# Streaming hybrid layer on one core: output weights split early and kept in DRAM, S5 units and their loads moved

## The chip, the cores and the metric

The kernel runs on one core of one Trainium2 chip. Times are device microseconds (us) of one execution. The five engines each take their instructions in order: TensorE (PE) multiplies, VectorE (DVE) and ScalarE (ACT) work elementwise, GpSimd (POOL) works elementwise and issues DMAs of its own, SyncE (SP) issues most of the DMAs. All DMAs run on the core's 16 DMA engines. The metric is the median time of several executions.

## The reference, cut to what matters

```python
h = rms_norm(x, norm_w)                       # x: 4096 prompt frames and 32 sample frames, 1024 wide
p = h @ w_in                                  # split into q/k/v, two gate logits, z_dn, u_s5, z_s5
qkv = silu(causal_conv4(p[:, :1536]))
o_dn = gated_delta_rule(l2(q), l2(k), v, g, beta, s0)   # 4 heads of 128, frames in sequence
o_dn = rms_norm(o_dn, dn_norm_w) * silu(z_dn)
y_s5 = s5_ssm(u_s5, ...)                      # 32 groups of 16, diagonal complex state
gy   = gelu(y_s5)
o_s5 = gy * sigmoid(gy @ glu_w + glu_b) * silu(z_s5)
y = rms_norm(x + concat([o_dn, o_s5]) @ w_out, final_norm_w)
```

All products are made from float16 pairs: a float32 operand is split into a high and a low half (`split`: ACT writes the high half, DVE the low one), and three matmuls of such halves (high by high, high by low, low by high) stand for one.

## The kernel before

The program is traced in Python and every loop is unrolled. A scheduler then lays out each engine's instructions at compile time: it takes the traced order as the priority (`high_priority` with a negative offset makes a block less urgent), and starts an instruction early where its own timing model says that the engine is free and the operands are there. On the chip the order of each engine is fixed: an instruction whose operand is late holds up everything behind it on its engine.

**Phase A** (`phase_a`, 0 to about 925 us of the span) normalizes x and stores it as pairs (`h_d`), splits the weights for it, runs the S5 recurrence (`s5_block`) and stores `gy_d`, and projects the two gate paths z (`zproj`: 24 matmuls of 512 columns for 128 rows, on operands fetched by DMA transposes `hz<-h_d`; line L549 is the transposes, L522 the matmuls). It takes the scale of `w_out` from a first reading (`wstat`). Behind the S5 recurrence it forms the bound of gy (`ma`, an all-partition maximum on POOL, and `pow2` on DVE, L153 to L155), the decay tables (`table`, 33 of them: matmuls L1047, DVE L1049, ACT L1051, a store `dm_d<-tdm`), and `phase_b1` splits the q, k, v and GLU weights and runs the first block of q, k, v. The z projections are traced with `high_priority(offset=-FILL)`, so they fill what the rest leaves of PE.

**Phase B** (`phase_b`) mixes two kinds of work by `Drive`, which keeps the order of PE: the streams of `chunks` (33 chunks of 128 frames in NP = 4 lanes, each urgent by its number) and the stream of `dense` (least urgent). A chunk has a front part (norms, two products, a triangular inverse) and a part that waits for the state S of the chunk before it and ends in L1651, which updates S. `dense` computes q, k, v of 16 blocks of 256 frames (`qkv`, L48 `pp<-h,wk` and so on; operands by DMA transposes in L1349), each allowed once the fronts of two earlier chunks are through, with two S5 output units behind each block while they last:

```python
late = units[len(units) - LATE:]          # 32 units (k, j), LATE = 8
units = units[:len(units) - LATE]
for b in list(range(1, SP)) + [-1] + list(range(SP, NB)):
    if b > 1:
        yield lambda: {2 * b - 4, 2 * b - 3} <= self.front
    yield from self.qkv(b) if b >= 0 else self.qkv_s()
    for u in units[:2] if b >= 0 else [(-1, 0)]:
        yield from self.s5out(*u)
```

With 24 units left by LATE, blocks 1 to 12 take two each and blocks 13 to 15 none; the last 8 follow the last block. Block -1 is the 32 sample frames (`qkv_s`), with a unit of its own.

One **unit** (`s5out`) takes 128 frames: it loads gy (`gyt<-gy_d`, L1446) and the gate (`zr<-z_d`, L1454), both from SP; splits gy into `gh` (L222 on ACT, L223 on DVE); transposes gy (4 matmuls, L52); multiplies by the GLU weight (12 matmuls of 512 columns, `pp<-wg,gh`); and closes with DVE L1462, L1468, L1470, ACT L1469, L1472, POOL L1473 and the store `m5_d<-zr` (L1475, in the trace `m_d<-zr`), which POOL issues. `gyt` and `zr` have two buffers, used in turn (`at = self.nu % 2`), and `gh` has one. `m5` lies in the buffer of `zr`, and the result `t` in that of `gyt`. So a buffer's next gy load can go once L1473 has read it, and the next gate load once the store has landed.

Behind the last block the **tail** follows: `c_weights` loads `w_out` (float32, 1 MB at a time into one staging buffer, L404) and splits it (8 splits, L222 and L223, `wo<-xw`), then the last 8 units, then the output projection of NE = 7 blocks (`out`, L48 `pp<-wo,mx`, transposes L1828 and L1830), while the last chunks run. The memory of the transposed operand `mx` is opened behind that of the staging buffer. **Phase C** does the other blocks of the output when the chunks are through.

Of the kernel before, what the change touches and what calls it, by code (L numbers as in the profile page):

```python
# [6 lines left out]
F32 = mybir.dt.float32  # L7
F16 = mybir.dt.float16
# [3 lines left out]
ALU = mybir.AluOpType  # L12
# [5 lines left out]
H = 4  # L18
# [3 lines left out]
TS = 32  # L22
# [3 lines left out]
FILL = 2000  # L26
# [4 lines left out]
KS = 4096.0  # L31
LATE = 8
SLACK = 1.5
# [46 lines left out]
class Trunk:  # L80
    def __init__(self, ctx, tc, io, T):
# [3 lines left out]
        nc = self.nc  # L85
# [37 lines left out]
        self.be_d = {"p": self.dram.tile([H, self.NC, 128], F32, name="be_d"), "s": self.dram.tile([H, 1, 128], F32, name="bes_d")}  # L123
        self.dm_d = [self.dram.tile([128, H, 128], F32, name=f"dm_d{c}") for c in range(self.NC + 1)]
        self.kp_d = self.dram.tile([16, 2, G, 240], F16, name="kp_d")

# [122 lines left out]
    def phase_a(self):  # L249
# [104 lines left out]
        self.e_gy = cst.tile([128, 2], F32, name="e_gy")  # L354
        self.pow2(ma, self.e_gy[:, 0:1], self.e_gy[:, 1:2])
        self.right.close()
# [7 lines left out]
        with self.tc.high_priority(offset=-250):  # L364
            for ci in order:
                self.table(ci)

        gcf = self.ngC.rearrange("t h c -> t (h c)")
# [670 lines left out]
    def table(self, ci):  # L1039
# [8 lines left out]
        dm = self.tbl.tile([128, H, 128], F32, name="tdm")  # L1048
        nc.vector.tensor_tensor(dm, ps, self.low.unsqueeze(1).to_broadcast([128, H, 128]), op=ALU.add)  # L1049
        for h in range(H):  # L1050
# [96 lines left out]
    def phase_b(self):  # L1147
# [31 lines left out]
        def dense():  # L1179
            units = [(k, j) for k in range(NB // 4) for j in range(8)]  # L1180
            late = units[len(units) - LATE:]
            units = units[:len(units) - LATE]
            for b in list(range(1, SP)) + [-1] + list(range(SP, NB)):
                if b > 1:
                    yield lambda: {2 * b - 4, 2 * b - 3} <= self.front
                yield from self.qkv(b) if b >= 0 else self.qkv_s()
                for u in units[:2] if b >= 0 else [(-1, 0)]:
                    yield from self.s5out(*u)
                if b >= 0:
                    units = units[2:]  # L1190
# [206 lines left out]
    def qkv_s(self):  # L1397
# [35 lines left out]
        yield 0  # L1433

    def s5out(self, k, j):

# [7 lines left out]
        gy = gy.rearrange("p (o i) -> p o i", o=4)[:, :, :m]  # L1444
        if k >= 0:
            nc.sync.dma_start(gy, self.gy_d[k].rearrange("o c t -> c o t")[:, :, 128 * j:128 * j + 128])  # L1446
        else:

            nc.sync.dma_start(gy, self.gys_d.rearrange("o c t -> c o t"))
            g = gh.rearrange("p (o i) -> p o i", o=4)[:, :, :m]  # L1450
            gp.tensor_copy(g.rearrange("p o (i s) -> p o s i", s=8), gy.rearrange("p o (s i) -> p o s i", s=8))
            gp.tensor_copy(gy, g)
        rows = (lambda d: d.rearrange("(i s) d -> s i d", s=8)[j]) if k >= 0 else (lambda d: d)
        nc.sync.dma_start(zr[:m], rows(self.z5_d[k] if k >= 0 else self.z5s_d))  # L1454
        gh = gh.bitcast(F16).rearrange("p (x o i) -> p x o i", x=2, o=4)[:, :, :, :m]
# [18 lines left out]
        dst = self.m5_d[k].rearrange("x (i s) d -> x s i d", s=8)[:, j] if k >= 0 else self.m5s_d  # L1474
        gp.dma_start(dst.rearrange("x t d -> t x d"), m5)  # L1475

    def load_be(self, ci):
# [320 lines left out]
    def c_weights(self):  # L1798
# [5 lines left out]
        self.nc.vector.tensor_scalar(self.uo, self.un["out"], self.em, 2.0 ** -5, op0=ALU.mult, op1=ALU.mult)  # L1804
        with ExitStack() as sc:
            self.wagain("out", self.pool(sc, "c_st", side="right"), self.w_o, 2)
        self.c_mx = self.pool(self.c0, "c_mx", 2, "right")
# [142 lines left out]
```

## Time and profile before

| | us |
|---|---|
| median of 3 runs | 2348.45 |
| runs | 2343.35, 2348.45, 2357.0 |
| the profiled execution | 2354.65 |
| its span in the profile | 2352.8 |
| PE busy | 2068.0 (88%) |
| DVE busy | 1440.2 (61%) |
| ACT busy | 1251.0 (53%) |
| POOL busy | 959.4 (41%) |

The profile is of one execution. Busy time is that of instructions in execution on an engine; where engines wait for each other, the rows tell the releaser, inferred from the semaphores. The granted clock of TensorE is given as a share of full speed: 1.00 is 2.4 GHz throughout a stretch, 0.50 is 1.2 GHz throughout.

### The profile page before, as it was taken

Reading aid. Unit: us, or ns where it says so; the run is one execution under the profiler, and the core shown is the slowest. Engines: PE = TensorE matmul, PEld = TensorE weight load, DVE = VectorE, ACT = ScalarE, POOL = GpSimd, SP = SyncE. Lnnn points to the kernel's source line nnn. Section 1 sums busy time; section 2 is a strip of 40 time slices with the busy share of each in tenths; the row PEclk is TensorE's granted clock in tenths of the full one; section 3 lists DMA queues with packets and bytes.
Section 4 is the critical chain, followed back from the end, with each engine's and each line's share of the span. In section 5 each row is a group of like instructions: output and inputs, shape, how many; then the busy total and the mean of one; then the engine's idle time right before and its main releaser. Section 6 shows DMA issues by size and latency. Waiting matters only on the chain.

```text
span 2352.8 us, 47799 instructions
## 1 busy us (share of the span) xinstructions
PE 2068.0 (88%) x18304; PEld 1492.9 (63%) x18304; DVE 1440.2 (61%) x3289; ACT 1251.0 (53%) x3695; POOL 959.4 (41%) x1444
## 2 busy tenths in 40 slices
PE   4688889888699998698799999989899868999998
PEld 3354677665467554487787778777778755554443
DVE  4685577559466222387687787778777786642223
ACT  5357546543386121376776677667677775431110
POOL 1344225212301012355666666666666675420000
PEclk9899899999899999799899999999999989999999
DMA  6169957765993644323133333322232145455542
GB/s 196 66 175 243 212 116 193 156 54 116 186 235 91 125 114 114 64 59 78 38 79 82 66 80 81 80 62 50 74 82 56 55 146 129 130 165 155 141 139 93
DMA packets 426349, 269.21 MB, mean 114 GB/s; under 512 B 344476, under 2 KB 379384, under 8 KB 425608
## 3 DMA queue, kind: packets, MB, share of 16 engines
q1 hardware_dynamic: 399400, 189.82, 37.1%
q0 software_dynamic: 21968, 67.69, 10.3%
q10 hardware_dynamic: 4752, 8.65, 1.2%
q8 instruction: 143, 2.34, 0.4%
q14 instruction: 86, 0.70, 0.1%
HBM read 102.27 MB, written 86.09 MB: 80 GB/s over the span
## 4 chain that ended last, share of the span: by engine, by line
PE 43%; issue 11%; ACT 7%; DMA 7%; DVE 6%; POOL 4%; SPq 1%; DVEq 0%; POOLq 0%; ACTq 0%
PE pp L48 23%; PE pz L522 9%; PE bk L48 7%; DMA gyt<-gy_d 3%; PE bk L52 2%; DVE acc L1384 2%; ACT jk L1555 2%; DMA dm_d<-tdm 1%; PE pt L1047 1%; DMA hz<-h_d 1%; DVE kn L1667 1%; DMA ab_d<-abt 1%; SPq L1349 1%; ACT acc L1382 1%; ACT br L1642 1%
## 5 line engine op out<-in xcount | busy, mean ns | idle before, releaser
L522 PE MATMUL pz<-wz,hz 128*128 128x512 f16 (+1 forms) x1464 | 385.7, 389 | 27.6 <-DMA hz<-h_d 25.5
L1384 DVE SCALAR_TENSOR_TENSOR acc<-pp,cwu,acc 128x256 f32<-128x256 f32 x540 | 252.9, 477 | 67.4 <-ACT acc L1382 60.6
L48 PEld LDWEIGHTS <-mx 128*128 128x128 f16 (+1 forms) x1584 | 152.3, 98 | 177.2 <-issue 1.6
L522 PEld LDWEIGHTS <-hz 128*128 128x128 f16 (+1 forms) x1464 | 143.4, 99 | 187.3 <-DMA hz<-h_d 33.3
L48 PE MATMUL pp<-h,wk 128*128 128x259 f16 (+1 forms) x1632 | 222.7, 276 | 0.1
L530 PE MATMUL pp<-wa,ht 128*128 128x260 f16 x1536 | 196.3, 284 | 27.1 <-ACT wa L222 10.4
L48 PE MATMUL pp<-h,wq 128*128 128x259 f16 (+1 forms) x1632 | 214.6, 273 | 0.5 <-DVE acc L1384 0.5
L48 PE MATMUL pp<-h,wv 128*128 128x259 f16 (+1 forms) x1632 | 209.9, 272 | 1.0 <-DVE acc L1384 1.0
L48 PE MATMUL po<-wo,mx 128*128 128x512 f16 (+1 forms) x912 | 197.2, 379 | 0.3 <-ACT acc L1219 0.3
L530 PEld LDWEIGHTS <-ht 128*128 128x128 f16 x1536 | 153.7, 101 | 57.1 <-issue 23.9
L48 PEld LDWEIGHTS <-wk 128*128 128x128 f16 x1632 | 156.5, 100 | 35.9 <-issue 8.8
L48 PEld LDWEIGHTS <-wq 128*128 128x128 f16 x1632 | 152.4, 99 | 27.6 <-issue 5.5
L48 PEld LDWEIGHTS <-wv 128*128 128x128 f16 x1632 | 148.5, 98 | 22.6 <-issue 1.6
L48 PE MATMUL pp<-wo,mx 128*128 128x512 f16 x672 | 152.0, 379 | 0.0
L556 POOL DMA_DIRECT2D z_d<-zt x64 | 36.8, 576 | 260.2 <-DVE zt L555 217.4
L1845 ACT ACTIVATE junk<-xt 128x1024 bf16<-128x1024 f32 (+1 forms) x19 | 20.1, 1056 | 176.4 <-issue 92.6
L48 PE MATMUL pp<-wg,gh 128*128 128x512 f16 (+1 forms) x396 | 104.2, 391 | 6.4 <-ACT gh L222 3.4
L555 DVE SCALAR_TENSOR_TENSOR zt<-zt,pz 128x512 f32<-128x512 f32 (+1 forms) x66 | 44.9, 680 | 102.0 <-ACT zt L554 101.3
L1382 ACT ACTIVATE acc<-pp,cwu 128x256 f32<-128x256 f32 x180 | 84.8, 482 | 38.6 <-PE pp L48 38.0
L48 PEld LDWEIGHTS <-a 128*128 128x128 f16 x1320 | 78.2, 98 | 37.3 <-issue 28.3
L1844 DVE SCALAR_TENSOR_TENSOR xt<-po,uo,xt 128x512 f32<-128x512 f32 (+1 forms) x38 | 28.5, 749 | 116.7 <-PE po L48 116.6
L948 POOL DMA_DIRECT2D gy_d<-vv x128 | 67.7, 535 | 78.7 <-ACT vv L943 40.3
(615 smaller groups left out, 5011.1 us busy)
## 6 DMA issues: line engine op xcount, KB each, us to landing
xn<-in_x SPq DMA_DIRECT2D x32, 512.0 KB, 4.5
h_d<-hl POOLq DMA_DIRECT2D x32, 512.0 KB, 5.4
z_d<-zt POOLq DMA_DIRECT2D x64, 256.0 KB, 3.6
xt<-in_x SPq DMA_DIRECT2D x18, 512.0 KB, 4.3
out_y<-xt SPq DMA_DIRECT2D x18, 512.0 KB, 3.6
dm_d<-tdm ACTq DMA_DIRECT2D x33, 256.0 KB, 3.7
dm<-dm_d SPq DMA_DIRECT2D x33, 256.0 KB, 2.9
gy_d<-vv POOLq DMA_DIRECT2D x128, 64.0 KB, 3.9
```

Source lines behind the costliest of these rows:

```text
L48: return self.nc.tensor.matmul(out, lhs, rhs, start=start, stop=stop)
L52: return self.nc.tensor.transpose(out, src, ident)
L522: self.nc.tensor.matmul(ps, a[x][:, c], w[:, y, c], start=c == 0 and x == y == 0, stop=c == K - 1 and x == 1)
L530: self.nc.tensor.matmul(pu[hf][:, :260], ht[x][:, c, :m], self.w_a[:, y, c, 260 * hf:260 * hf + 260], start=c == 0 and x == y == 0, stop=c ...
L555: nc.vector.scalar_tensor_tensor(zt, zt, 1.0, pz, op0=ALU.add, op1=ALU.mult)
L556: nc.gpsimd.dma_start(rows(dst[0][blk]) if blk >= 0 else dst[1], zt)
L948: gp.dma_start(gy[s], gn[16 * s:16 * s + 16, :, :128])
L1047: nc.tensor.matmul(ps[:, h], self.ident[:k, p:p + 1].to_broadcast([k, 128]), gc, start=True, stop=True)
L1382: nc.scalar.activation(acc, ps[:, 0:n], AF.Copy, scale=cw[:, e, 0:1])
L1384: v.scalar_tensor_tensor(acc, ps[:, j:j + n], cw[:, e, j:j + 1], acc, op0=ALU.mult, op1=ALU.add)
L1555: act.activation(junk, src[:, h], AF.Square, accum_out=out[:, h:h + 1])
L1844: v.scalar_tensor_tensor(xt[:m, sl], ps, self.uo[:m], xt[:m, sl], op0=ALU.mult, op1=ALU.add)
```

## The change

1. `w_out` is split in phase A. Behind the decay tables, at the low priority of the z projections, eight pieces are loaded by SP (two staging buffers), split by ACT and DVE into one buffer `ho`, and stored by POOL into a DRAM tensor `wo_d`. `c_weights` then only loads the finished pairs from it, eight DMAs of 512 KB on SP, with no staging buffer. The new pool `b_wo` (12 KB in each partition) lies behind the pools of the tables in SBUF and is closed with them.
2. The `pow2` of the S5 bound is traced behind the tables and its first instruction is tied behind the last table's DVE instruction.
3. LATE goes from 8 to 4, and four units (EARLY) are traced ahead of block 2, before the wait for the fronts of chunks 0 and 1. Blocks 1 to 12 still take two units each, and four remain for the tail.
4. The loads of a unit stand in `s5load`. The first four units load at their own start, from SP, as before. From the third unit on, a unit ends with the loads for the unit two behind it (`useq` is the order of all 33): the gy load issued by POOL, behind the unit's own store, and the gate load by SP.

```diff
--- before.py
+++ after.py
@@ -29,7 +29,8 @@
 SB = 2
 Z0 = 3
 KS = 4096.0
-LATE = 8
+LATE = 4
+EARLY = 4
 SLACK = 1.5
 
 
@@ -122,6 +123,7 @@
         self.m5s_d = self.dram.tile([2, TS, 512], F16, name="m5s_d")
         self.be_d = {"p": self.dram.tile([H, self.NC, 128], F32, name="be_d"), "s": self.dram.tile([H, 1, 128], F32, name="bes_d")}
         self.dm_d = [self.dram.tile([128, H, 128], F32, name=f"dm_d{c}") for c in range(self.NC + 1)]
+        self.wo_d = [self.dram.tile([128, 2, 1024], F16, name=f"wo_d{k}") for k in range(8)]
         self.kp_d = self.dram.tile([16, 2, G, 240], F16, name="kp_d")
 
 
@@ -352,7 +354,6 @@
         v.tensor_single_scalar(mx, mx, 91.0, op=ALU.add)
         ma = self.allmax(mx, 1, "g")
         self.e_gy = cst.tile([128, 2], F32, name="e_gy")
-        self.pow2(ma, self.e_gy[:, 0:1], self.e_gy[:, 1:2])
         self.right.close()
         self.tbl = self.pool(bld, "b_tbl", 3)
         self.pt = self.pool(bld, "b_pt", 2, psum=True)
@@ -364,6 +365,17 @@
         with self.tc.high_priority(offset=-250):
             for ci in order:
                 self.table(ci)
+
+        wp = self.pool(bld, "b_wo")
+        with self.tc.high_priority(offset=-FILL):
+            for k in range(8):
+                f = wp.tile([128, 1024], F32, name="xo", bufs=2)
+                hl = wp.tile([128, 2, 1024], F16, name="ho")
+                nc.sync.dma_start(f, io["w_out"][:, k])
+                self.split(hl[:, 0], hl[:, 1], f, self.ws["out"][:, k:k + 1])
+                nc.gpsimd.dma_start(self.wo_d[k], hl)
+        self.after(v.tensor_single_scalar(ma, ma, 2.0 ** -100, op=ALU.max), self.last_tdm)
+        self.pow2(ma, self.e_gy[:, 0:1], self.e_gy[:, 1:2])
 
         gcf = self.ngC.rearrange("t h c -> t (h c)")
         mark = self.last_exp
@@ -1046,7 +1058,7 @@
             p = h * n + c
             nc.tensor.matmul(ps[:, h], self.ident[:k, p:p + 1].to_broadcast([k, 128]), gc, start=True, stop=True)
         dm = self.tbl.tile([128, H, 128], F32, name="tdm")
-        nc.vector.tensor_tensor(dm, ps, self.low.unsqueeze(1).to_broadcast([128, H, 128]), op=ALU.add)
+        self.last_tdm = nc.vector.tensor_tensor(dm, ps, self.low.unsqueeze(1).to_broadcast([128, H, 128]), op=ALU.add)
         for h in range(H):
             self.last_exp = nc.scalar.activation(dm[:, h], dm[:, h], AF.Exp, bias=self.ngC[:, h, ci:ci + 1])
             self.after(self.last_exp, self.last_gelu)
@@ -1178,9 +1190,14 @@
 
         def dense():
             units = [(k, j) for k in range(NB // 4) for j in range(8)]
+            self.useq = units[:2] + [(-1, 0)] + units[2:]
             late = units[len(units) - LATE:]
             units = units[:len(units) - LATE]
             for b in list(range(1, SP)) + [-1] + list(range(SP, NB)):
+                if b == 2:
+                    for u in units[:EARLY]:
+                        yield from self.s5out(*u)
+                    units = units[EARLY:]
                 if b > 1:
                     yield lambda: {2 * b - 4, 2 * b - 3} <= self.front
                 yield from self.qkv(b) if b >= 0 else self.qkv_s()
@@ -1432,6 +1449,14 @@
             self.blk[-1, nm] = dst[:, H * i:H * i + H]
         yield 0
 
+    def s5load(self, k, j, at, eng):
+        m = 128 if k >= 0 else TS
+        gy = self.rm["gyt"][:, at].rearrange("p (o i) -> p o i", o=4)[:, :, :m]
+        eng.dma_start(gy, self.gy_d[k].rearrange("o c t -> c o t")[:, :, 128 * j:128 * j + 128] if k >= 0 else
+                      self.gys_d.rearrange("o c t -> c o t"))
+        rows = (lambda d: d.rearrange("(i s) d -> s i d", s=8)[j]) if k >= 0 else (lambda d: d)
+        self.nc.sync.dma_start(self.rm["zr"][:m, at], rows(self.z5_d[k] if k >= 0 else self.z5s_d))
+
     def s5out(self, k, j):
 
 
@@ -1442,16 +1467,13 @@
         gy, zr, gh = self.rm["gyt"][:, at], self.rm["zr"][:, at], self.rm["gh"][:, 0]
         t, m5 = gy, zr
         gy = gy.rearrange("p (o i) -> p o i", o=4)[:, :, :m]
-        if k >= 0:
-            nc.sync.dma_start(gy, self.gy_d[k].rearrange("o c t -> c o t")[:, :, 128 * j:128 * j + 128])
-        else:
-
-            nc.sync.dma_start(gy, self.gys_d.rearrange("o c t -> c o t"))
+        if self.nu <= 4:
+            self.s5load(k, j, at, nc.sync)
+        if k < 0:
+
             g = gh.rearrange("p (o i) -> p o i", o=4)[:, :, :m]
             gp.tensor_copy(g.rearrange("p o (i s) -> p o s i", s=8), gy.rearrange("p o (s i) -> p o s i", s=8))
             gp.tensor_copy(gy, g)
-        rows = (lambda d: d.rearrange("(i s) d -> s i d", s=8)[j]) if k >= 0 else (lambda d: d)
-        nc.sync.dma_start(zr[:m], rows(self.z5_d[k] if k >= 0 else self.z5s_d))
         gh = gh.bitcast(F16).rearrange("p (x o i) -> p x o i", x=2, o=4)[:, :, :, :m]
         self.split(gh[:, 0], gh[:, 1], gy, self.gs)
         pt = self.pb.tile([128, 512], F32, name="pp")[:m]
@@ -1473,6 +1495,8 @@
         gp.tensor_tensor(m5[:, 1], t, m5[:, 0], op=ALU.subtract)
         dst = self.m5_d[k].rearrange("x (i s) d -> x s i d", s=8)[:, j] if k >= 0 else self.m5s_d
         gp.dma_start(dst.rearrange("x t d -> t x d"), m5)
+        if 2 < self.nu < len(self.useq) - 1:
+            self.s5load(*self.useq[self.nu + 1], at, gp)
 
     def load_be(self, ci):
 
@@ -1802,8 +1826,8 @@
         self.w_o = wt.tile([128, 2, 8, 1024], F16, name="wo")
         self.uo = wt.tile([128, 1], F32, name="uo")
         self.nc.vector.tensor_scalar(self.uo, self.un["out"], self.em, 2.0 ** -5, op0=ALU.mult, op1=ALU.mult)
-        with ExitStack() as sc:
-            self.wagain("out", self.pool(sc, "c_st", side="right"), self.w_o, 2)
+        for k in range(8):
+            nc.sync.dma_start(self.w_o[:, :, k], self.wo_d[k])
         self.c_mx = self.pool(self.c0, "c_mx", 2, "right")
 
     def phase_c(self):
```

## Rows read from the trace of the kernel before

**Rows 1.** Stretches: PE, PEld, DVE, ACT, POOL busy; PE's clock; DMA share; GB/s.

```profile
700.00:925.00 225.00, 224.96 (x1449) 134.18 (x1447) 82.81 (x202) 70.00 (x152) 28.73 (x53) 1.00 0.49 114
925.00:951.00 26.00, 4.89 (x145) 4.42 (x141) 6.40 (x9) 5.38 (x18) 14.84 (x23) 0.62 0.73 131
951.00:1027.00 76.00, 63.15 (x575) 49.48 (x576) 39.51 (x95) 38.11 (x120) 27.35 (x41) 0.86 0.23 43
1027.00:1885.00 858.00, 783.07 (x9183) 681.15 (x9180) 650.62 (x1565) 618.09 (x1997) 552.46 (x788) 0.97 0.29 69
1885.00:1962.00 77.00, 51.83 (x483) 37.80 (x480) 63.35 (x110) 53.06 (x147) 51.37 (x55) 0.82 0.62 167
1962.00:2110.00 148.00, 147.85 (x1123) 82.47 (x1120) 82.09 (x166) 62.56 (x181) 58.87 (x85) 0.99 0.47 125
```

**Rows 2.** ACT's waits, 1027 to 1885 us: total us, times, longest.

```profile
ACT gh L222 <- DMA gyt<-gy_d: 45.3, 11, 6.6
```

**Rows 3.** Timeline of one S5 buffer from 1188 us: start, length, engine, line.

```profile
1188.22 1.15 POOL L1473 TENSOR_TENSOR zr<-gyt,zr 128x512 f16<-128x512 f32 x1
...
1189.39 0.36 SPq L1446 DMA_DIRECT2D gyt<-gy_d  x1
...
1189.66 0.77 POOL L1475 DMA_DIRECT2D m_d<-zr  x1 [0.30 <-POOL zr L1473]
...
1192.32 0.72 ACT L222 ACTIVATE gh<-gyt,gs 128x512 f16<-128x512 f32 x1 [1.34 <-DMA gyt<-gy_d]
```

**Rows 4.** Timelines of SP, POOL and ACT at a longer stall, from 1306 us.

```profile
1306.98 10.19 SPq L1349 DMA_TRANSPOSE h<-h_d  x1
1317.27 0.52 SPq L1446 DMA_DIRECT2D gyt<-gy_d  x1
...
1312.54 1.16 POOL L1473 TENSOR_TENSOR zr<-gyt,zr 128x512 f16<-128x512 f32 x1 [1.81 <-ACT zr L1472]
...
1322.63 0.72 ACT L222 ACTIVATE gh<-gyt,gs 128x512 f16<-128x512 f32 x1 [6.58 <-DMA gyt<-gy_d]
```

**Rows 5.** PE's waits, 1027 to 1885 us, the two longest in total.

```profile
PE bk L48 <- DVE T L1716: 12.2, 15, 2.7
PE bk L48 <- ACT tp L1519: 7.2, 6, 3.3
```

**Rows 6.** POOL's store of a unit, 1027 to 1885 us: busy, mean ns.

```profile
L1475 POOL DMA_DIRECT2D m_d<-zr x22 | 16.4, 747 | 3.6 <-POOL zr L1473 3.6
```

**Rows 7.** DMA issues: size of each, median us to landing.

```profile
vb<-z_d POOLq DMA_DIRECT2D x32, 256.0 KB, 3.0
...
xn<-in_w_out SPq DMA_DIRECT2D x8, 512.0 KB, 5.9
```

**Rows 8.** The tail's output weights by tile: ns min/median/max, first and last start.

```profile
L48 PE MATMUL pp<-wo,mx x112: 376/379/379, 1968.7 to 1999.9; 128*128 128x512 f16 x112
...
L223 DVE SCALAR_TENSOR_TENSOR wo<-xw,ws_out,wo x8: 1273/1281/2172, 1904.3 to 1943.2; 128x1024 f16<-128x1024 f32 x8
```

**Rows 9.** The chain that ended last, its longest piece: start, us, what.

```profile
2110.75 33.67 PE pp L48 x156
```

**Rows 10.** DVE's updates of the state by chunks 20, 24 and 31.

```profile
1730.43 1.11 DVE L1651 SCALAR_TENSOR_TENSOR S_p<-S_p,egl,bk 128x128 f32<-128x128 f32 x4
...
1847.55 1.11 DVE L1651 SCALAR_TENSOR_TENSOR S_p<-S_p,egl,bk 128x128 f32<-128x128 f32 x4
...
2110.85 1.11 DVE L1651 SCALAR_TENSOR_TENSOR S_p<-S_p,egl,bk 128x128 f32<-128x128 f32 x4
```

**Rows 11.** Timelines of SP and ACT at the sample unit, from 937 us.

```profile
937.38 9.21 SPq L1349 DMA_TRANSPOSE h<-h_d  x1
...
951.25 0.40 ACT L222 ACTIVATE gh<-gyt,gs 128x128 f16<-128x128 f32 x1 [16.06 <-POOL gyt L1452]
```

**Rows 12.** Timeline of PE at the decay tables, from 626 us.

```profile
626.34 2.08 PE L1047 MATMUL pt<-gcp,ident 128*128 128x128 f32 x8 [16.34 <-DVE tdm L1049]
...
644.03 6.00 PE L1047 MATMUL pt<-gcp,ident 128*128 128x128 f32 x32 [4.24 <-DVE mm L155]
```

## The prediction

> **What bounds the kernel now.** I read the busy time by stretches first. From 700 to 925 us PE is never idle and its clock is full; from 1962 to 2110 us nearly so. Between them three stretches lose time [rows 1]: the start of the chunks (925 to 1027 us, PE busy 68 of 102 us at clocks of 0.62 and 0.86), the long middle (1027 to 1885 us, busy 783 of 858 us at 0.97), and the head of the tail (1885 to 1962 us, busy 52 of 77 us at 0.82). Elsewhere only PE's work counts, so a gain is idle time or half-speed time taken out of one of these three, and a loss is time put into a stretch where PE is full.
>
> Then the waits. In the middle ACT stands still 45.3 us in all for a gy load, 11 times, up to 6.6 us [rows 2]: the next block's first split of gy stands in ACT's order right behind where the load was thought to land. In the tail the output weights are what is late: the last low half starts at 1943.2 us, and the first output matmul only at 1968.7 us [rows 8]. At the start the sample unit's split holds ACT for 16.06 us: SP is busy 9.21 us with a transpose before it issues the small load [rows 11].
>
> **The tail.** At a clock of 0.82 the 51.83 us of PE in its first 77 us are some 42.5 us of full-speed work; 34.5 us are lost [rows 1]. The change takes out the eight splits, the staging buffer's four rounds, and four of eight units. What is left is eight loads of 512 KB. A load of that size of the same weights took 5.9 us to land [rows 7]; the DMA's 167 GB/s of this stretch [rows 1] would move 4.2 MB in 25 us, so the weights are there some 25 us into the stretch, near 1910 us, instead of 1944 us. The transposes of `mx` no longer wait for the staging buffer, but go behind these loads on SP. I take the first output matmul at 1915 us. A unit's 12 matmuls cost 2.6 us, at 33.67/156 = 0.216 us each [rows 9], so eight units are 21 of the 42.5 us and the chunks' work the rest, 0.28 us per us. In 30 us there are then 10.4 us of units and 8.4 us of chunks: 11 us lost. PE's work from 1885 us to the end of the chunks is 42.5 + 0.99 x 147.85 = 189 us; less 10.4 moved away it is 178.5, and with 11 us lost it ends at 2075 us instead of 2110 us.
>
> That holds only if the chunks are through by then. Chunk 31 ends at 2110.85 us, and phase C opens behind it [rows 10]. From chunk 20 to 24 a chunk took 29.3 us; from 24 to 31, with the outputs between, 37.6 us. Seven chunks at 29.3 us end at 2053 us, at 37.6 us where they end now. With 10 us less of other work and no splits in ACT's and DVE's order I take 33.5 us: 2082 us. So **tail: -28 us**, from -47 (PE loses nothing: 2063 us) to 0 (the present pace).
>
> **The start.** Four units go there. Their PE work is 10.4 us, against 102 - 0.62 x 4.89 - 0.86 x 63.15 = 45 us lost there now [rows 1]. But most of this is lost before the sample unit's load lands at 951 us, and that load keeps its place behind SP's transpose. The four units come after it, two buffers in turn; each brings ACT a split that can wait. If each waits as in the middle (45.3/11 = 4.1 us) and none of the PE work is absorbed, they cost 27 us; if all fits, nothing. After 951 us some 22 us are lost (76 - 0.86 x 63.15), so half of the work should fit, with a few us of waiting: **+8 us**, bounds 0 and +27.
>
> **The middle.** Is the load earlier? L1473 frees the buffer at 1189.4 us, and SP issues the load there and then; POOL would issue the store first, at 1189.66 us for 0.77 us, and the load behind it [rows 3]. In the longer stall the buffer was free at 1313.7 us and SP, in its transpose until 1317.2 us, issued at 1317.27 us; the split started at 1322.63 us [rows 4]. So the load goes out up to 3 us earlier where SP was held and about 1 us later where it was not: nearly the same on the mean. "Two units ahead" is where it stood already. What may change is the split's place in ACT's order, since the plan now sees a store and a load on POOL ahead of it; that can take perhaps half of 45.3 us of standing. PE's two longest waits on what ACT and DVE do behind it come to 19.4 us [rows 5], which is the most that I give this. Against it stands POOL's own time: a gy load of 512 runs, where the unit's store of 256 rows holds POOL 0.747 us [rows 6], so about 1.2 us for each of 22 units, 26 us on an engine busy 552 of 858 us [rows 1]; PE's two longest waits name no POOL instruction, so most of it is covered, and without the cover it is at worst a third, 8 us. A load issued by POOL is no slower by itself: `vb<-z_d` lands in 3.0 us [rows 7]. The gate load still waits on SP for the store to land, with the next transposes and the chunks' loads behind it, as before. **-7 us**, from -19 to +8.
>
> The Trainium skill (DMA: Bandwidth & Descriptors, section Issuing engines are not separate DMA queues) speaks against this part: starting DMAs on several engines "will only save the time on the sequencer it takes to initiate the DMA". The trace agrees as far as it goes, since SP's issue took 0.36 us [rows 3]; by that rule the middle would stand at nothing and the sum below at -18.
>
> **Phase A.** The early splitting brings eight times 1.28 us to DVE [rows 8], about as much to ACT, eight loads on SP, eight stores on POOL and 8.4 MB to the DMAs. Each store waits on POOL for both halves of its split, with the stores of z behind it; each load from the third on waits on SP for a staging buffer, with the transposes for z behind it. ACT is busy 70 and DVE 83 of 225 us there, so the engines have room; PE has none, and any z projection that comes late costs in full [rows 1]. Operands are two ahead, 24 x 0.216 = 5.2 us each, which covers short holds. The tables before it already make PE wait 16.34 us behind their stores and 4.24 us behind a small DVE operation of the bound's group [rows 12]; with the bound and what hangs on it behind the tables the 4.24 us may go. I set one short hold of 6 us against 4: **+2 us**, from -4 to +20 (three rounds each late by one projection's 5.2 us, and 4 us more). The moved bound itself costs nothing: its users are the units and the chunks' scales, all behind the tables. `b_wo` gives its memory to phase B's pools, whose first tiles must wait for the last store; that is covered as long as the splits end before 925 us.
>
> **Sum**: -28 + 8 - 7 + 2 = -25 us. The profiled execution took 2354.65 us, 6 us above the median of 2348.45 us; from 2354.65 it gives 2330, and as a median **2323 us**.
>
> **Rivals** (times as medians).
> The stalls of the middle go entirely, and the four units fit in the start: -28 - 19 + 2 = -45, 2303 us. For it: each stall sits on one load alone [rows 2]. Against it: the buffer is freed no earlier. 0.15.
>
> The queue doesn't matter: POOL's issue changes neither landing nor ACT's order, so that the change does not do in the middle what it says; -28 + 8 + 2 = -18, 2330 us. For it, the load that SP issues as the buffer comes free [rows 3]; against it, the one that SP holds [rows 4]. 0.12. It is what the Trainium skill's page DMA: Bandwidth & Descriptors would make of the move.
>
> The chain of chunks bounds the tail: outputs start earlier, but chunk 31 ends no sooner, at 37.6 us a chunk, and PE runs dry before phase C. 0 + 8 - 7 + 2 = +3, 2351 us. For it: that pace [rows 10]. Against it: PE was full there, and the pace was 29.3 us with full blocks of q, k, v between. 0.15.
>
> The other side, slower: the staging of `w_out` sits in SP's order ahead of transposes for z. SP waits for a staging buffer until the split before it, and PE has one projection's cover. With a load of 5.9 us [rows 7], a split of 2.6 (two halves like DVE's) and a store of the same size as the load, a round is 14.4 us, so a full hold costs 14.4 - 5.2 = 9 us; six rounds wait so (two buffers are free at first): 55 us, and -25 - 2 + 55 = +28, 2376 us. At three rounds it is level with before, from five slower by over 0.5%. For it: PE has no idle time there; against it: engines with two thirds idle time split promptly. 0.08.
>
> **Numbers.** The forecast has 0.50. A difference under 0.5%, 12 us, is about what a measurement here cannot tell from none. Faster by more: forecast, first and second rival, 0.50 + 0.15 + 0.12 = 0.77; the same: the third, 0.15; slower 0.08. The range is 2288 to 2352 us: below the first rival by most of the tail's own bound, above up to the third's; the slower rival and a little at the low end stay out.
>
> **What would show it.** Right: the first `pp<-wo,mx` within 35 us of the last block of q, k, v; no `wo<-xw` behind phase A; chunk 31 about 28 us sooner after chunk 24; ACT's wait on gy loads in the middle cut but not gone; the stretch from 700 us to the first dm load not longer than 225 us. Wrong: PE idle between the last early output and phase C (third rival), waits of PE on hz in phase A (fourth), ACT held 4 us or more by each early unit between 951 and 1027 us, or POOL as the releaser of PE's waits in the middle.

## The result, and the profile after

The changed kernel takes 2321.97 us (median of four runs, 2318.2 to 2327.94) against 2347.88 us before: a ratio of 0.9872, 95% interval 0.9845 to 0.9899. The profiled execution took 2318.2 us with a span of 2316.5 us, 36.3 us less than the profiled one before. Part of these 36 us is no effect of the change, as will be seen.

The stretches of the changed kernel, cut at its own marks; columns as in [rows 1]:

```profile
700.00:925.00 225.00, 223.08 (x1439) 131.58 (x1438) 90.92 (x234) 72.97 (x155) 34.14 (x64) 1.00 0.56 130
925.00:951.00 26.00, 4.80 (x142) 4.33 (x137) 8.07 (x9) 5.21 (x18) 14.35 (x20) 0.64 0.86 133
951.00:1051.50 100.50, 80.59 (x733) 59.83 (x734) 59.10 (x128) 55.40 (x171) 48.16 (x66) 0.91 0.29 71
1051.50:1881.00 829.50, 775.87 (x9151) 680.71 (x9150) 660.63 (x1564) 614.60 (x1977) 566.50 (x804) 0.98 0.32 71
1881.00:1923.00 42.00, 27.58 (x268) 20.09 (x266) 26.16 (x57) 26.25 (x81) 30.07 (x39) 0.79 0.92 247
1923.00:2109.00 186.00, 184.67 (x1376) 102.34 (x1376) 95.34 (x202) 74.19 (x226) 68.85 (x101) 0.99 0.44 118
```

Busy time times clock is full-speed work; the rest of a stretch is lost. In the start 50 of 126.5 us are lost, against 45 of 102 before; in the middle about 69, against 98; from the last block to phase C 24 of 228, against 39 of 254 (clocks have two digits, so the middle is good to some 4 us, the others to about 1). The start holds 19 us more work: the four units and what of blocks and chunks came with them. The tail holds 11 us less. The row of the tail before, from its last block to phase C:

```profile
1891.80:2145.60 253.80, 228.31 (x1703) 130.81 (x1702) 151.33 (x283) 115.83 (x325) 109.22 (x145) 0.94 0.55 151
```

ACT's wait for gy loads in the middle (total, times, longest), 45.3 us in [rows 2]:

```profile
ACT gh L224 <- DMA gyt<-gy_d: 7.9, 8, 2.1
```

PE's long wait at the tables, 626.34 us in [rows 12], ends here at

```profile
618.68 2.08 PE L1059 MATMUL pt<-gcp,ident 128*128 128x128 f32 x8 [15.19 <-DVE tdm L1061]
```

The tail: the output matmuls and weight loads by tile (ns min/median/max, first and last start), DVE's longest wait in its head, SP's loads of the gate and the last chunk's update:

```profile
L49 PE MATMUL pp<-wo,mx x672: 376/380/635, 1923.0 to 2107.2; 128*128 128x512 f16 x168
L1830 SPq DMA_DIRECT2D wo<-wo_d x8: 602/771/4829, 1883.1 to 1893.5; - x8
```

```profile
DVE zr L1484 <- DMA zr<-z_d: 7.3, 1, 7.3
```

```profile
1918.53 1.04 SPq L1458 DMA_DIRECT2D zr<-z_d  x2
...
2102.70 1.12 DVE L1675 SCALAR_TENSOR_TENSOR S_p<-S_p,egl,bk 128x128 f32<-128x128 f32 x4
```

All eight weight loads are issued by 1893.5 us, and at 11.6 to 16.2 us to landing they are there near 1910 us. The first output matmul starts at 1923.0 us. Last come the gate loads of two units: the stores that free their buffers go out at 1892.22 and 1897.73 us, but SP, in the transposes of `mx` for some 23 us, issues them at 1918.53 us, and DVE and then PE (5.8 us) wait for them. Chunk 31 ends 8 us earlier than in [rows 10], but only 6 us ahead of phase C (2109 us), where before it was 35 us (2145.6 us).

### The profile page after: what moved, and what is told of

Read it like the earlier page. It is cut to its first block, busy times and chain, and to the rows that moved or that the text cites. A ratio compares the mean times of both kernels' runs of the same rounds, so it can differ in the third digit from the quotient of the medians.

```text
span 2316.5 us, 47857 instructions
## 1 busy us (share of the span) xinstructions
PE 2053.1 (89%) x18304; PEld 1486.0 (64%) x18304; DVE 1443.1 (62%) x3290; ACT 1250.8 (54%) x3695; POOL 983.3 (42%) x1481
## 4 chain that ended last, share of the span: by engine, by line
PE 39%; issue 10%; DVE 9%; ACT 5%; DMA 4%; POOL 4%; SPq 0%; DVEq 0%; POOLq 0%; ACTq 0%
PE pp L49 23%; PE bk L49 8%; PE pz L534 5%; PE bk L53 2%; DVE acc L1401 2%; ACT jk L1579 1%; DMA gyt<-gy_d 1%; DVE kn L1691 1%; DMA hz<-h_d 1%; PE po L49 1%; DVE gyt L1492 1%; DMA h<-h_d 1%; DMA dm_d<-tdm 0%; ACT acc L1399 0%; DVE ubd L1746 0%
## 5 line engine op out<-in xcount | busy, mean ns | idle before, releaser
L49 PE MATMUL pp<-h,wk 128*128 128x259 f16 (+1 forms) x1632 | 217.5, 272 | 0.1
L1579 ACT ACTIVATE jk<-bk 128x128 bf16<-128x128 f32 x264 | 74.9, 284 | 38.9 <-PE bk L53 33.1
```

Source lines behind the costliest of these rows:

```text
L49: return self.nc.tensor.matmul(out, lhs, rhs, start=start, stop=stop)
L1579: act.activation(junk, src[:, h], AF.Square, accum_out=out[:, h:h + 1])
```

## The experiments

All were compared with the kernel before on the same chip (its medians there 2356 to 2361 us), so ratios count. Two theories of the middle: **place** (the gain comes from where the split of gy stands in ACT's order) and **queue** (it comes from the load's move off SP). This table, from PE's timelines, cuts each profile at the same events: the end of PE's long wait at the tables; the last z matmul; the first matmul of block 3; the last of v of block 15; the first of phase C. The column "lost in the tail" is the tail less PE's busy time in it times its clock. All but the ratio is in us. Where an expectation names a time, it reckons from the 2348 us of the result, so a run's ratio times 2348 us is what it has to be held against.

| run | ratio | phase A | start | middle | tail | lost in the tail | ACT's gy waits |
|---|---|---|---|---|---|---|---|
| before | 1 | 297.8 | 102.8 | 864.9 | 253.8 | 39 | 45.3 |
| the change | 0.9872 | 305.3 | 127.5 | 829.5 | 228.1 | 24 | 7.9 |
| E1 tie alone | 0.9932 | 296.5 | 103.1 | 847.0 | 254.2 | 38 | 0 |
| E2 change, loads on SP | 0.9953 | 306.9 | 117.7 | 857.9 | 227.5 | 25 | 36.1 |
| E3 part 4 alone | 0.9934 | 295.2 | 100.9 | 853.1 | 258.8 | 42 | 15.9 |
| E4 change, no early units | 1.0011 | 307.8 | 102.3 | 856.2 | 256.3 | 38 | 15.7 |
| E5 change, no part 1 | 0.9920 | 297.9 | 127.6 | 837.3 | 240.9 | 40 | 8.5 |
| E6 change, units in blocks 13, 14 | 0.9891 | 310.1 | 101.6 | 860.1 | 230.3 | 29 | 15.0 |
| E7 tie and LATE 4 | 0.9872 | 296.9 | 101.8 | 858.3 | 236.2 | 38 | 0 |
| E8 change and tie | 0.9889 | 305.9 | 127.1 | 835.5 | 230.8 | 30 | 0 |
| E9 change, SP, tie | 0.9831 | 309.6 | 117.5 | 825.2 | 230.2 | 29 | 0 |
| E10 E7, part 1 behind the tables | 0.9881 | 311.8 | 99.1 | 863.5 | 221.4 | 16 | 0 |
| E11 E10 with LATE 2 | 0.9880 | 311.5 | 100.4 | 863.5 | 221.7 | 17 | 0 |
| E12 E9 without part 1 | 0.9943 | 297.1 | 117.7 | 852.5 | 239.9 | 38 | 0 |

The intervals are within 0.002 to 0.004 of the ratio. From phase C to the end it is 207 to 208 us in every run. PE's wait at the tables ended between 618.7 (the change) and 634.5 us (E1). Up to there PE, ACT and POOL run the same instructions in the same order in every profile, before and after: what stands ahead of it varies from one execution to the next, and 7.7 of the 36.3 us between the two profiles came from there.

**E1, the place alone.** In the kernel before:

```diff
-                        nc.scalar.activation(dst, dst, AF.Copy, scale=self.sq["p"])
+                        self.qmark = nc.scalar.activation(dst, dst, AF.Copy, scale=self.sq["p"])
...
-        self.split(gh[:, 0], gh[:, 1], gy, self.gs)
+        self.split(gh[:, 0], gh[:, 1], gy, self.gs, marks=(self.qmark, None))
```

> The kernel before with one edit: each unit's high half of gy is ordered on ACT behind the last q of the block before it; loads, queues, unit places and output weights are untouched. First theory (place): the middle gained because ACT no longer stands at a gy load that has just gone out, so the tie alone takes ACT's 45.3 us of such waits below 10 us and PE's lost time between the start of block 2 and the last block from about 99 us to about 70: 2348 - 25 to 30 = 2318 to 2323 us. Rival (queue): the gain came with the load's move off SP; then ACT's waits go, but PE stays where it was, 2343 to 2350 us.

2342.36 us, 0.9932 (0.9909 to 0.9954). ACT's 45.3 us of waits are gone, the middle is 17.9 us shorter, the other stretches stay. With no load moved, the tie is worth 16 us of time (2332 us on the scale of the expectation), half of what the changed middle shows: less than the place theory asked for and more than the queue theory allowed. The tie also changes the rest of the plan (see E12), so E1 alone does not show that the whole gain comes from the waits.

**E2, the queue undone.**

```diff
-            self.s5load(*self.useq[self.nu + 1], at, gp)
+            self.s5load(*self.useq[self.nu + 1], at, nc.sync)
```

> The changed kernel with the two-ahead gy loads issued by SP instead of POOL. Place theory: the time follows where the split stands on ACT. If it comes back to right behind the load, ACT's waits come back towards 45 us and the middle is up to 30 us longer, 2335 to 2352 us; if it stays where it is, 2317 to 2327 us, though SP issues the loads up to 10 us late behind its transposes. Queue theory: loads are held on SP by transposes and by waits for the units' stores, ACT waits as before wherever the split stands, 2340 to 2352 us.

2348.19 us, 0.9953 (0.9925 to 0.998), 2337 us on the scale of the expectation; its interval reaches into the ranges of both theories, so the time does not decide. ACT's waits in the middle are back:

```profile
ACT gh L224 <- DMA gyt<-gy_d: 36.1, 10, 5.4
```

Yet SP holds these loads no more than POOL did: in the middle they go out within 2.3 us of L1495's end (POOL's in the change 1.0 to 3.1 us behind it), and the split stands again right behind where they land. So place again, and the middle is 28 us longer. But the start is 10 us **shorter** than with POOL. Most of that is work that stands elsewhere: the start of the change, then that of E2:

```profile
924.00:1051.50 127.50, 86.39 (x897) 64.93 (x897) 67.17 (x137) 61.20 (x189) 62.51 (x85) 0.85 0.41 83
```

```profile
935.50:1053.20 117.70, 80.32 (x818) 60.67 (x818) 64.64 (x121) 53.26 (x155) 53.83 (x73) 0.81 0.39 83
```

E2 does 79 matmuls less there, 65 us of full-speed work against 73; 53 us are lost against 54. POOL's issue does come later: POOL issues a load of the change behind the unit's store and other work (POOL's timeline; the buffer is free when L1495 ends):

```profile
976.67 1.16 POOL L1495 TENSOR_TENSOR zr<-gyt,zr 128x512 f16<-128x512 f32 x1
977.79 1.15 POOL L1715 TENSOR_TENSOR a<-br,bd 128x512 f16<-128x512 f32 x1
978.90 1.15 POOL L1719 TENSOR_TENSOR al<-br,ah 128x512 f16<-128x512 f32 x1
...
980.47 0.77 POOL L1497 DMA_DIRECT2D m_d<-zr  x1
981.23 0.77 POOL L1455 DMA_DIRECT2D gyt<-gy_d  x1
```

and SP in E2, 0.03 and 0.6 us behind the end of L1495:

```profile
986.16 0.36 SPq L1455 DMA_DIRECT2D gyt<-gy_d  x1
...
990.20 0.38 SPq L1455 DMA_DIRECT2D gyt<-gy_d  x1
```

**E3, part 4 alone** (LATE 8, no early units, output weights and bound as before).

```diff
-LATE = 4
-EARLY = 4
+LATE = 8
+EARLY = 0
...
-        for k in range(8):
-            nc.sync.dma_start(self.w_o[:, :, k], self.wo_d[k])
+        with ExitStack() as sc:
+            self.wagain("out", self.pool(sc, "c_st", side="right"), self.w_o, 2)
```

> The kernel before with the loads two ahead alone (gy by POOL): LATE is 8, no early units, output weights and the bound as before. Both theories of the middle: about 30 us of PE's lost time go there and nothing else changes, 2315 to 2325 us, as quick as the whole change. The forecast's own size for this part was -7 us, 2341 us. If the middle gained in truth because work was moved into the start, nothing, 2345 to 2352 us.

2345.54 us, 0.9934 (0.991 to 0.9958). The middle gives 11.8 us, not 30, and there the forecast's -7 us was the nearer. The time, 2332 us on the scale of the expectation, lies between the two. The tail is 5 us longer with these loads.

**E4, no early units.**

```diff
-LATE = 4
-EARLY = 4
+LATE = 8
+EARLY = 0
```

> The changed kernel without the early units: LATE 8, EARLY 0; the other parts stay. Theory that the 25 us by which block 2 comes later are mostly work moved there (19 us) from the middle and the tail, and 5 us more of lost time: block 2 starts near 953 us again, the tail has four units more (10 us of PE) and the middle what else had moved, 2317 to 2325 us. Rival, that the early units simply hold up the start by 25 us: 2322 - 25 + 10 = 2307 us. Second rival, that without them the tail loses its head start: the tail is 10 us of units and up to 11 us of lost time longer, 2330 us or more.

2359.83 us, 1.0011 (0.9986 to 1.0035): all that was gained is gone, and only the second rival comes near. The tail is as long as before although the weights are split early, because the outputs are traced behind the units: the first output matmul starts 80.4 us behind the last block, as the last unit's L1484 ends (1977.26 to 1978.01 us). The stretch, and PE's longest wait in it, which ends at 1940.33 us and is for a gate load that SP issues behind the transposes of `mx`:

```profile
1897.60:1978.00 80.40, 55.52 (x496) 37.91 (x495) 51.42 (x106) 44.88 (x137) 51.33 (x70) 0.83 0.68 174
```

```profile
PE pp L49 <- DVE zr L1484: 9.2, 1, 9.2
```

So with eight units part 1 buys nothing in the tail, and costs 10 us in phase A.

**E5, no part 1.** The pool `b_wo` is left out, and `c_weights` loads and splits as before:

```diff
-                self.split(hl[:, 0], hl[:, 1], f, self.ws["out"][:, k:k + 1])
-                nc.gpsimd.dma_start(self.wo_d[k], hl)
...
-        for k in range(8):
-            nc.sync.dma_start(self.w_o[:, :, k], self.wo_d[k])
+        with ExitStack() as sc:
+            self.wagain("out", self.pool(sc, "c_st", side="right"), self.w_o, 2)
```

> The changed kernel without part 1: the output weights are loaded and split behind the last block, as before; the early units, the loads two ahead and the moved bound stay. Theory that the tail's gain comes from its four units fewer, and that part 1 costs phase A about 10 us (from the end of PE's long wait at the tables to the last z matmul 305 to 308 us with it, 295 to 298 without): phase A is 9 us shorter, and the tail at most 13 us longer if the weights (54 us behind the last block, before) take the place of the four units (42 us): -9 to +4 us against the change, a ratio of 0.983 to 0.989. Rival, that the weights bound the tail, as the forecast had it: the tail is as long as before less the four units' 10 us of work, +15 us less the 9: a ratio of 0.990 or more.

2343.7 us, 0.992 (0.9897 to 0.9942): the rival's ratio. Phase A is 7.4 us shorter and the tail 12.8 us longer, as the theory had it, which is 5 us; the rest of the 11 us lies in a middle 7.8 us longer, with the same tracing there. The tail's 12.8 us, against "at most 13" and "15", cannot tell the two apart, but its rows can. DVE's splits, and the tails of E4 and of this run to phase C:

```profile
L224 DVE SCALAR_TENSOR_TENSOR wo<-xw,ws_out,wo x8: 1269/1280/3625, 1912.9 to 1949.7; 128x1024 f16<-128x1024 f32 x8
```

```profile
1897.60:2153.90 256.30, 230.10 (x1703) 131.19 (x1702) 133.78 (x271) 108.14 (x316) 109.09 (x152) 0.95 0.57 149
```

```profile
1896.10:2137.00 240.90, 216.57 (x1647) 126.13 (x1646) 138.10 (x265) 111.00 (x318) 104.58 (x142) 0.93 0.55 146
```

The last unit's last GLU matmul starts at 1936.8 us, the last split at 1949.7 us and the first output matmul at 1957.4 us, 61 us behind the last block: with four units left, late weights (and the transposes of `mx`, which SP issues behind their loads, from 1942.84 us on) are what comes last, as the rival has it. Early weights alone (E4) leave 38 us of the tail lost and fewer units alone 40 us, against 39 us before; only the two together, as in the change, bring it to 24. What fewer units alone take off the tail is work done elsewhere.

Phase A at 297.9 us with the moved bound says that part 2 costs nothing. It gains nothing either: the 4.24 us of [rows 12] are gone, but PE's waits at the tables come to 22.1 us in all, with 15.9 in the long one, against 21.6 with 16.3 before.

**E6, the four units in blocks 13 and 14.**

```diff
-EARLY = 4
+EARLY = 0
```

> The changed kernel with EARLY 0 and LATE 4: the four units go to blocks 13 and 14 instead of ahead of block 2. Against the run without early units (LATE 8, ratio 1.001) the tail should be 28 us shorter, as it is in the change. Theory that the start gives the early units room for nothing: in the middle PE is full, they cost there their 10 us of work and the time is 18 us better than without, a ratio of 0.993. Rival, that the middle has room as well (PE idle 53 to 61 us there): 28 us better, 0.989.

2336.26 us, 0.9891 (0.9872 to 0.991): the rival's figure. Against E4 the tail is 26 us shorter and the middle only 4 us longer. Units need not go into the start. That the middle has room in general is not shown: the same move makes it 11 us longer in E7 than in E1.

**E7, tie and LATE 4.** The two edits of E1 in the kernel before, and

```diff
-LATE = 8
+LATE = 4
```

> The kernel before with two edits of a line each: the tie of the gy split on ACT behind the last q of the block before (alone 0.993), and LATE 4, so that four units go from the tail to blocks 13 and 14. Nothing is split early, no queue is changed. If the number of units sets the tail: the tail 25 us shorter less up to 13 us for the weights, the middle 18 us shorter by the tie and up to 10 us longer by the units: -20 to -33 us, a ratio of 0.986 to 0.9915. Rival, that the weights, split as late as before, bound the tail: only the units' 10 us move, nothing is gained on the sum, and the ratio is that of the tie, 0.993 to 0.995.

2330.0 us, 0.9872 (0.9846 to 0.9899): these lines alone are as fast as the whole change. With late weights the tail is 17.6 us shorter, but 38 us of it are lost, as before; the middle holds the units' work and is 11 us longer than in E1.

**E8, change and tie** (the edits of E1 in the changed kernel).

> The changed kernel with the tie added. Place theory: ACT's last 8 us of waits on gy loads in the middle go, with little behind them, 0 to -8 us against the change: a ratio of 0.984 to 0.987. Rival, that the change's middle gained by the queue as well as by the place, and the tie only moves the split later than its user needs it: the same or worse, 0.987 to 0.990.

2336.17 us, 0.9889 (0.9865 to 0.9914), not to be told from the change: the rival's figure, though the interval reaches the place theory's. The last 8 us of ACT's waits were worth nothing that can be seen.

**E9, change, loads on SP, tie** (the edits of E1 and E2 in the changed kernel).

> The changed kernel with the two-ahead gy loads on SP, as in the run that was 0.995, and with the tie of the gy split on ACT. Place theory: the SP loads cost only because the split stood right behind them again (ACT waited 36 us); with the tie the stretch from the last z matmul to the last block is as long as in the change with or without tie, 957 to 965 us, against 975.6 with SP alone: a ratio of 0.986 to 0.990. Queue theory: SP's loads are late whatever ACT does, 973 us or more, a ratio of 0.993 to 0.997.

2321.57 us, 0.9831 (0.9796 to 0.9866): the lowest ratio of all, below what place had asked for, though its interval overlaps the change's and touches E8's. With the place fixed POOL's queue is not needed. The start is 10 us shorter as in E2 (117.5 us), again with 68 to 78 matmuls less than in E8 and the change, and the middle, which holds them, is 4 to 10 us shorter.

**E10 and E11, part 1 behind the tables.** E7, with part 1 (not part 2) and

```diff
+                self.split(hl[:, 0], hl[:, 1], f, self.ws["out"][:, k:k + 1], marks=(self.last_exp, self.last_tdm))
```

> The kernel before with the tie, LATE 4, and part 1 with one difference: the eight splits of the output weights are ordered on ACT and DVE behind the last decay table. Theory that part 1 costs phase A 10 us because its splits stand between the tables: phase A is 295 to 300 us again, the tail 228 to 231 us as with early weights, against 236 us without: 5 to 8 us better than tie and LATE 4 alone, a ratio of 0.983 to 0.985. Rival, that it costs by its DMAs and by SP's and POOL's queues, wherever the splits stand: phase A 304 to 310 us, a ratio of 0.987 to 0.989.

2334.0 us, 0.9881 (0.9848 to 0.9915). Phase A is 311.8 us: the rival's side, beyond its figure. The tail is 221.4 us, 15 us shorter than in E7 and shorter than the theory asked for, and the middle 5 us longer. The splits no longer stand between the tables, and now PE waits for operands of z:

```profile
750.00:945.00 195.00, 184.16 (x1090) 98.97 (x1087) 58.87 (x132) 45.48 (x75) 35.62 (x66) 0.99 0.61 150
```

```profile
PE pz L532 <- DMA hz<-h_d: 7.4, 7, 1.6
```

Then the same with LATE 2:

```diff
-LATE = 4
+LATE = 2
```

> The same with LATE 2: blocks 1 to 15 take two units each and the tail has two. If the tail is set by its units: its head is some 20 us shorter and holds 5 us less of work, the middle has 5 us more, 8 to 15 us better than with LATE 4, a ratio of 0.977 to 0.981. Rival, that the chain of chunks bounds the tail now (chunk 31 came 211 to 230 us behind the last block in every run so far): phase C opens no sooner than 217 us behind the last block, and the middle's 5 us go against it, a ratio of 0.982 to 0.986.

2332.45 us, 0.988 (0.9841 to 0.9919): outside both, on the rival's side. But this run puts neither to the test. Block 15's two units are traced behind its v, so they stand in the tail either way; only their order against the loads of the weights changes. The tails of E10 and E11 hold the same matmuls, and so do the middles (9313 each):

```profile
1907.90:2129.30 221.40, 209.86 (x1639) 120.77 (x1638) 121.14 (x255) 100.03 (x302) 94.60 (x136) 0.98 0.56 157
```

```profile
1901.80:2123.50 221.70, 208.62 (x1638) 120.53 (x1637) 120.84 (x255) 99.67 (x302) 94.06 (x136) 0.98 0.58 157
```

PE is busy for all but 12 and 13 us of these tails, the shortest of all. Chunk 31 comes 206.6 and 206.9 us behind the last block, sooner than in any other run; why was not tried.

**E12, E9 without part 1** (the edits of E5 in E9).

> The changed kernel with the gy loads on SP and the tie (0.983), and without part 1: the output weights are loaded and split behind the last block, as before. If the stretches add as in the runs so far: phase A 295 to 298 us instead of 309.6, the stretch from the last z matmul to the last block 943 us again, the tail 236 to 241 us instead of 230: 1 to 9 us better, a ratio of 0.979 to 0.983. Rival, that part 1 gives back in the tail all that it costs in phase A once the middle is short: 0.983 to 0.986.

2344.01 us, 0.9943 (0.9924 to 0.9962): outside both. Phase A (297.1) and tail (239.9 us) are as expected; the middle is 27 us longer than in E9, though the traced program there is the same. Five blocks of the middle, in the order before, the change, E1, E12, E9, each from its own trace:

```profile
1379.60:1712.30 332.70, 303.46 (x3525) 261.50 (x3524) 254.61 (x600) 235.65 (x757) 211.81 (x300) 0.98 0.30 71
```

```profile
1384.20:1701.80 317.60, 301.64 (x3538) 262.20 (x3536) 259.12 (x603) 236.61 (x759) 222.01 (x311) 0.98 0.34 76
```

```profile
1380.50:1703.90 323.40, 304.52 (x3521) 262.70 (x3520) 255.72 (x601) 239.35 (x755) 213.71 (x300) 0.97 0.33 75
```

```profile
1394.00:1717.40 323.40, 304.64 (x3522) 263.72 (x3520) 257.06 (x601) 239.50 (x756) 213.79 (x300) 0.97 0.31 75
```

```profile
1398.30:1705.80 307.50, 296.32 (x3522) 258.76 (x3521) 250.64 (x601) 236.37 (x755) 214.15 (x301) 0.99 0.34 79
```

PE's longest waits there, in E12 and then in E9:

```profile
PE bk L49 <- ACT sp L1534: 5.1, 5, 1.0
PE bk L49 <- DVE ubd L1737: 3.6, 5, 0.7
PE bk L49 <- DVE knT L1535: 3.0, 5, 0.6
```

```profile
PE bk L49 <- DVE Tf L1788: 3.1, 5, 0.6
PE bk L49 <- DVE p L1755: 2.8, 10, 0.3
PE bk L49 <- ACT br L1666: 2.0, 5, 0.4
```

These waits come five times, or ten: with the tie and SP's loads the scheduler's plan falls into a cycle of one block. In E12 ACT's order repeats itself block for block, instruction for instruction, and the cycle is that of E1, 64.7 us a block; E7, E10 and E11 run at that pace too. E9's is another, 61.5 us, and repeats itself but for a few instructions. Loads at a unit's start (E1) or two units ahead (E12) are the same cycle; E9 differs from E12 in part 1 alone, hundreds of us earlier.

So ACT's waits do not size the middle by themselves. With none of them left, PE's lost time there runs from 65 us (E9) to 93 us (E12); E3, with 15.9 us of them, loses 94, and the change, with 7.9, 69.

## Why the prediction was right, and where its steps were not

The total holds: forecast -25 us, measured -25.9 us between the medians. So does the outline of the mechanism: the tail gains by weights and units together, the middle by a split that stands later in ACT's order, and the start and phase A pay for part of it. By stretches the two profiles say +7.5 (phase A), +24.7 (start), -35.4 (middle), -25.7 (tail): -29 us. Three of four terms (start, middle, phase A) were mis-sized, and their errors cancel, so that the total came out this near is in part luck. Of the prediction's signs of being right, three came: no split of the weights behind phase A, ACT's gy wait cut but not gone, and 224.8 us from 700 us to the first dm load. Two did not: the first output matmul within 35 us of the last block (42), and chunk 31 some 28 us sooner after chunk 24 (1 us).

- **Tail, -28 us.** Measured -25.7: 11 us of work done elsewhere and 15 us of lost time, against 10.4 and some 18 in the forecast. The size is right, but two of its reasons fell. The weights are not all that was late [rows 8]: before, the first output matmul (1968.7 us) stands among the GLU matmuls of the last unit (to 1972.3 us), and by E4 early weights alone give nothing. With the four units gone the late weights are last (E5), so each part works only with the other. The first output matmul comes 42 us behind the last block, not 30, on SP's late gate loads. And chunk 31 comes no sooner: from chunk 24 it takes 263.3 us in [rows 10] and here 262.5 us (1840.17 to 2102.70). The forecast let phase C open behind chunk 31; in the kernel before 35 us of outputs still lay between them. So the third rival was right on the pace and wrong on the time.
- **Start, +8 us.** Measured +24.7, near the bound of +27. 19 us of it is work that came there, which the middle and the tail are spared; 5 us is lost time. The forecast held that half of the units' work would fit in, and did not see that work of blocks and chunks would come with them. With SP's loads (E2, E9, E12) the start is 10 us shorter than with POOL's (the change, E8, E5: 117.5 to 117.7 against 127.1 to 127.6 us), but by their rows 6 to 8 us of that is work that stands elsewhere, and 1 to 4 us is lost time that POOL's issue may have cost. Only one early split held ACT for over 4 us (5.51 us).
- **Middle, -7 us.** Measured -35.4, beyond the bound of -19. Some 6 us is work moved away, 29 us lost time. The step that failed is the cap by PE's two longest waits [rows 5]. The place was named rightly and the landing is no earlier, as was said: E1 gets 17.9 us with a tie alone, and E2, which puts the split back by the queue alone, loses 28. What comes on top is the order that the plan falls into (E12 against E9: 27 us with the same tracing), which no row of waits could size; how much of the change's own 29 us is that order stays open.
- **Phase A, +2 us.** The two profiles show +7.5 from the end of the wait at the tables, hidden by an earlier stage that ran 7.7 us shorter. Runs with part 1 need 305 to 312 us, runs without 295 to 298: about 11 us. So part 1 gives in the tail (10 to 15 us with four units: the change against E5, E9 against E12, E10 against E7) what it costs here, or little more. The fourth rival's hold in SP's order did not come in the change; E10 shows the nearest to it.
- **The queue (second rival).** It held that POOL's issue changes neither the landing nor ACT's order. E2 differs from the change by the queue alone and has ACT's waits back and the longer middle: the queue matters by the place that the plan then gives the split, as the forecast said it might. With the place tied, POOL's loads (E8, 0.9889) bring nothing over SP's (E9, 0.9831). The price of a load was put too high: it took POOL 0.77 us, not the estimated 1.2. The Trainium skill (DMA: Bandwidth & Descriptors, section Issuing engines are not separate DMA queues) promises no more than the issuer's own time from a second engine. E8 and E9 agree that POOL's issue brings nothing of its own.

Of the parts: the four units less shorten the tail by some 15 us alone, all of it work that stands elsewhere, and by some 26 with part 1; part 1 is worth about its own cost, part 2 nothing, and part 4 alone 15 us (E3), which the tie gives as well (E1). Why the plan takes the slower cycle in E12 and the faster in E9 stays open; it was not tried with the order of E9 held fixed.

## What to carry to other kernels

Where a scheduler writes the engines' orders at compile time, a stall on a load can be cured by the place of the instruction that waits, with one order tie, before any load is moved; and a DMA issued by a working engine stands in that engine's queue. Cut two traces at the same events and split each stretch into work and lost time: here terms of +25, -35 and -26 us would else be read as costs and gains, when 19 us of the first is work that was only moved. Two changes that each take no lost time out of a stretch alone can take 15 us out together, when either one leaves the other as what comes last. A total that comes out as forecast proves no term of its sum, and parts measured one at a time need not add when every edit makes a new plan.

## What the runs showed that was not expected

Two orders of the same work per block, both with no wait of ACT on a load, run at 61.5 and 64.7 us a block: 1.6 of the 3.2 us are PE's own busy time (304.5 to 304.6 us against 296.3 for five blocks), as its granted clock there is 0.97 against 0.99. And the same instructions ahead of the tables ended up to 16 us apart (618.7 to 634.5 us) between executions, more than some of the parts weigh.
